# The long sequence's input passes and norm written in front of the last six tiles of the short projection

## The chip, the cores and the metric

The kernel runs on one core of one Trainium2 chip. The metric is the device time of one execution in microseconds, and the number compared is the median of several executions.

## The reference, cut to what matters

Two groups of requests go through the same trunk with shared weights: a long sequence of 1024 positions and a short one of 512, each with 16 meta tokens in front. Only the first part of the layer matters here: the input norm, the combined projection in 18 column tiles of 128, and the attention that reads it.

```
def rms_norm(x, g):
    x32 = x.astype(jnp.float32)
    y = x32 * lax.rsqrt(jnp.mean(x32 * x32, axis=-1, keepdims=True) + NORM_EPS)
    return (y * g.astype(jnp.float32)).astype(x.dtype)

def mixer_sublayer(x, ang_a, ang_b, layer, g_mix, w_in, ...):
    n = rms_norm(x, g_mix)
    proj = n @ w_in                       # 1024 -> 2304 columns
    qa, ka, va, qb, kb, vb = jnp.split(proj, cuts, axis=-1)
    qa = rope_rotate(rms_norm(qa, g_qnorm_a), ang_a)
    ka = rope_rotate(rms_norm(ka, g_knorm_a), ang_a)
    ...                                   # grouped-query attention: 8 heads on 2 K/V heads
    qb = rope_rotate(qb, ang_b)
    kb = rope_rotate(kb, ang_b)
    ...                                   # differential attention: two softmax maps per head
    mix = jnp.concatenate([oa, ob], axis=-1)
    return x + mix @ w_out
...                                       # ConvGLU sublayer, final norm
```

## The kernel before, in words

Activations lie with the feature dimension on the 128 partitions and the positions along the free dimension. The code calls the long sequence s=0 (1040 positions with the meta tokens) and the short one s=1 (528 positions). Every large product runs in three matmul passes on values split in a high and a low part (`mm3`, lines L121, L122, L123: high weight by high x, high weight by low x, low weight by high x), over eight blocks of the contraction, so one product is 24 matmuls. A scheduler decides the order of the instructions on each engine from the order in which the program writes them, taking what is written first when several are ready; each engine then runs its own list strictly in order.

`projection` is a generator that is written once and run for each sequence. It has three parts. First come the input passes, for each of eight feature blocks: a load of x, `xhi` (L234, ScalarE), `xlo` (L235, VectorE), a square (L238, ScalarE) and, for the long sequence, a running sum of the squares in `acc` (L245, GpSimd). Then comes the norm: the first product (`first_ps`, tile KA, first chunk of positions) is written ahead of it, and for each chunk a matmul with `ones_d` sums `acc` over the partitions (L255), ScalarE and VectorE turn it into a reciprocal root (`rsqrt_newton`, L103 to L107) and one VectorE instruction scales all of `rstd` (L257). Only then can the first product leave PSUM, since its eviction `t = ps * rstd` (L312) reads the scaled `rstd`. The long sequence has three chunks, of 384, 384 and 272 positions, the short one two, of 256 and 272. Third come the 18 column tiles, in the order KA, VA, QA, VB, QA+1, ... VB+3, then KB, QB, KB+1, QB+1, ... KB+3, QB+3, with a `yield` after each chunk. The q and k tiles of group A have a norm of their own (L318, L103 to L107, L321) and a rotation, and their results go to memory; those of KB and QB only a rotation.

The program writes the whole projection of the short sequence, then merges two generators: the short sequence's attention and the long sequence's projection, which is to fill TensorE while the softmax of the attention runs. PSUM has two buffers `ps_mm` (long projection: its products, its norm sums, the sums of the head norms, the transposed values), three `ps_s` (products of the short projection, scores of the attention), two `ps_t` and one `ps_o`. The scores are moved out of `ps_s` by VectorE (L433); probabilities are normalised by VectorE (L508), transposed by TensorE (L456) and split again (L114 on ScalarE, L115 on VectorE) before they meet V (L470, L471).

Two orders are forced by hand: the long sequence's input passes stand behind the short sequence's norm (`g.norm_of_short`), and the long sequence's first product stands behind product number 13 of the short projection (`g.short_products`).

Of the kernel before, what the change touches and what calls it, by code (L numbers as in the profile page):

```python
# [74 lines left out]
def behind(g, *ins):  # L75

    es = ExitStack()
    for i in ins:
        es.enter_context(g.tc.issue_after(i))
    return es  # L80
# [13 lines left out]
def pool(ctx, g, name, bufs, side):  # L94
    return ctx.enter_context(g.tc.tile_pool(name=name, bufs=bufs, side=side, reuse_waits="tile"))


def rsqrt_newton(g, tp, out, src, w, eps=None):

    nc = g.nc  # L100
    eps = g.eps if eps is None else eps
    y = tp.tile([P, w], F32, name="rs_y", tag="rs_y", bufs=1)
    nc.scalar.activation(y, src, AF.Ln, bias=eps)  # L103
    nc.scalar.activation(y, y, AF.Exp, scale=-0.5)
    last = nc.scalar.activation(out, y, AF.Square).ins
    nc.vector.scalar_tensor_tensor(out=out, in0=src, scalar=eps, in1=out, op0=ALU.add, op1=ALU.mult)
    nc.vector.scalar_tensor_tensor(out=out, in0=out, scalar=-3.0, in1=y, op0=ALU.add, op1=ALU.mult)  # L107
    return last
# [17 lines left out]
def dense(g, ps, w, xhi, xlo, c0, cw, order=range(KT)):  # L126

    for i, k in enumerate(order):
        last = mm3(g, ps, *block(w, k), xhi[k][:, c0:c0 + cw], xlo[k][:, c0:c0 + cw], i == 0, i == KT - 1)
    return last  # L130
# [66 lines left out]
def projection(ctx, g, s, side, tag, tag2):  # L197
# [9 lines left out]
    xlo = [xp.tile([P, n], F32R, name=f"xlo{k}") for k in range(KT)]  # L207
    rstd = xp.tile([P, n], F32, name="rstd")
    products = []

    def load_tables(which):
        out = []
        for i in range(2):
            tb = xp.tile([P, n], F32, name="rope", tag="rope", bufs=2 if s == 0 else 4)
            nc.sync.dma_start(out=tb, in_=g.rope_in[2 * which + i][:, :n])
            out.append(tb)
        return out
# [3 lines left out]
    with tc.tile_pool(name=f"ps{s}", bufs=2, side=side, reuse_waits="tile") as sp:  # L221
        if s == 1:
            ms = [g.psum.tile(P, cw, tag2) for _, cw in chunks]
        else:
            acc = sp.tile([P, n], F32, name="acc", bufs=1)
        for k in range(KT):
            x = sp.tile([P, n], F32, name="x", tag="x", bufs=2 if s == 0 else 8)
            nc.sync.dma_start(out=x, in_=g.xT[s][k * P:(k + 1) * P, :])
            gk = g.vec[:, V_GMIX + k:V_GMIX + k + 1]
            with ExitStack() as order:  # L230

                for ins in g.norm_of_short:
                    order.enter_context(tc.issue_after(ins))
                nc.scalar.activation(xhi[k], x, AF.Copy, scale=gk)  # L234
                nc.vector.scalar_tensor_tensor(out=xlo[k], in0=x, scalar=gk,  # L235
                                               in1=xhi[k].bitcast(F32), op0=ALU.mult, op1=ALU.subtract)
                sq = acc if k == 0 and s == 0 else x
                nc.scalar.activation(sq, x, AF.Square)  # L238
            if s == 1:
                for ps, (c0, cw) in zip(ms, chunks):  # L240
                    nc.tensor.matmul(ps, lhsT=g.ones_d, rhs=x[:, c0:c0 + cw], start=k == 0, stop=k == KT - 1)
            elif k:
                for c0, cw in chunks:
                    a = acc[:, c0:c0 + cw]
                    nc.gpsimd.tensor_tensor(out=a, in0=a, in1=x[:, c0:c0 + cw], op=ALU.add)  # L245
        c0, cw = chunks[0]
        first_ps = g.psum.tile(P, cw, tag)
        with behind(g, *g.short_products):
            products.append(dense(g, first_ps, first, xhi, xlo, c0, cw))
        for i, (c0, cw) in enumerate(chunks):  # L250
            if s == 1:
                ps = ms[i]
            else:
                ps = g.psum.tile(P, cw, tag2)
                nc.tensor.matmul(ps, lhsT=g.ones_d, rhs=acc[:, c0:c0 + cw], start=True, stop=True)  # L255
            last = rsqrt_newton(g, sp, rstd[:, c0:c0 + cw], ps, cw)
        scaled = nc.vector.tensor_scalar(out=rstd, in0=rstd, scalar1=-0.5, scalar2=None, op0=ALU.mult)  # L257
        g.norm_of_short = [last, scaled.ins]
    es = ExitStack()
    bp = pool(ctx, g, f"pb{s}", 2, side)  # L260
    tp = pool(es, g, f"pt{s}", 2, side)
# [106 lines left out]
    for i in range(4):  # L368
        for j in (KB + i, QB + i):
            w = load_weight(g, wp, g.w_in[j], ahead=1 + s, lo_engine=nc.gpsimd if s == 0 else None)  # L370
            for c0, cw in chunks:
# [3 lines left out]
                    follow()  # L375
                rotary(j, c0, cw, ps, *tab)
                yield 24 * cw
    if s == 1:

        g.short_products = products[13:14]  # L380


def attention(ctx, g, s, side):
# [191 lines left out]
def add_square(g, tp, acc, h, j, c0, cw, eng, bufs=2):  # L575

    nc = g.nc
    hs = h[:, j, c0:c0 + cw]
    if j == 0:
        nc.scalar.activation(acc, hs, AF.Square)  # L580
    else:
        sq = tp.tile([P, cw], F32, name="sq", tag="sq", bufs=bufs)
        nc.scalar.activation(sq, hs, AF.Square)
        eng.tensor_tensor(out=acc, in0=acc, in1=sq, op=ALU.add)
# [163 lines left out]
def conv_glu(ctx, g, s, st, side, wp, wb, gb):  # L748
# [20 lines left out]
    for f0 in range(0, NFF, G):  # L769
# [59 lines left out]
        def finish(c0, acc, sums):  # L829
            rs = rstd[:, 1 + c0:1 + c0 + cw]  # L830
            if sums:
                rsqrt_newton(g, op, rs, acc, cw)
            else:
                mean_rsqrt(g, op, rs, acc, cw)
            for k in range(KT):
                y = op.tile([P, ob, cw], F32, name="y", tag="y", bufs=YB if s == 1 else 4) if k % ob == 0 else y
                hs, gk = h[:, k, 1 + c0:1 + c0 + cw], g.gain[:, V_GFIN + k:V_GFIN + k + 1]
                if k % 4 == 3:
                    nc.scalar.activation(y[:, k % ob], hs, AF.Copy, scale=gk)
                    nc.gpsimd.tensor_tensor(out=y[:, k % ob], in0=y[:, k % ob], in1=rs, op=ALU.mult)  # L840
                else:
                    nc.vector.scalar_tensor_tensor(out=y[:, k % ob], in0=hs, scalar=gk, in1=rs,
                                                   op0=ALU.mult, op1=ALU.mult)
                if (k + 1) % ob == 0:
                    (nc.gpsimd if s == 1 else nc.sync).dma_start(out=yv[:, k + 1 - ob:k + 1, c0:c0 + cw], in_=y)

        waiting = None
        for c0 in range(0, N, cw):
# [3 lines left out]
            for j in range(KT):  # L852
# [5 lines left out]
                else:  # L858
                    add_square(g, op, acc, h, j, 1 + c0, cw, nc.gpsimd if j < PADD else nc.vector, ob)
                if j == LAG and waiting:  # L860
                    finish(*waiting)
# [372 lines left out]
def merge(a, wa, b, wb, ahead=0.0):  # L1234

    done = [float(ahead), 0.0]
    while True:
        i = 0 if b is None or done[0] / wa <= done[1] / wb else 1
        try:
            done[i] += next((a, b)[i])  # L1240
        except StopIteration:
            if i == 0:
                break
            b = None


def drain(gen):
    for _ in gen:
        pass


LAG = 5
NPRE = 4
FPRE = 12
# [16 lines left out]
def trunk_kernel(ctx, tc, g):  # L1271
# [67 lines left out]
    g.norm_of_short, g.short_products = [], []  # L1339

    g.splits = []
    with ExitStack() as es:
        drain(projection(es, g, 1, "right", "s", "t"))
    g.splits = None
    with ExitStack() as es0:
        p0 = projection(es0, g, 0, "left", "mm", "mm")
        with ExitStack() as es1:
            merge(attention(es1, g, 1, "right"), R1[0], p0, R1[1])
        drain(p0)
# [92 lines left out]
```

## Time and profile before

| | before |
|---|---|
| device time, median of 3 executions | 2129.21 us (2128.84, 2129.21, 2135.24) |
| the profiled execution: its own time | 2138.1 us |
| the profiled execution: span, first to last instruction | 2136.3 us |
| mean granted TensorE clock | 0.982 of full speed |
| TensorE busy, share of the span | 2051.1 us, 96% |
| VectorE busy | 1724.1 us, 81% |
| ScalarE busy | 1156.8 us, 54% |
| GpSimd busy | 582.7 us, 27% |

The busy shares are means over stages that differ. What is to be read is the stretch from about 117 us, where the last six tiles of the short projection start, to about 200 us, where the merge of the short attention with the long projection is under way. All times in the views are microseconds from the start of the span. In the views PE is TensorE's matmuls, PEld its weight loads, DVE VectorE, ACT ScalarE, POOL GpSimd, and SPq the queue that issues the transfers; PEclk is the granted clock as a share of 2.4 GHz, so 0.50 is 1.2 GHz.

### The profile page before, as it was taken

To read this page: it belongs to the slowest core of one execution; us is meant where nothing else is said; L and a number is where in the kernel's file an instruction comes from. 1 tells how busy PE (TensorE), PEld (TensorE's weight loads), DVE (VectorE), ACT (ScalarE), POOL (GpSimd) and SP (SyncE) were. 2 spreads that over 40 slices of the span, in tenths; PEclk is the share of its full clock that TensorE was granted. 3 is DMA by queue.
4 is the path that set the end of the run, shared out by engine and by line. 5 is a ranking of instruction groups with operands and counts; after the bars stand their busy time and mean duration, and the time that the engine had idled before them with its cause. 6 is when DMAs were issued, how large, how long until landed. Compare 5 with 4: busy or idle time off the path is not lost.

```text
span 2136.3 us, 35264 instructions
## 1 busy us (share of the span) xinstructions
PE 2051.1 (96%) x12302; PEld 1833.1 (86%) x12302; DVE 1724.1 (81%) x3786; ACT 1156.8 (54%) x2253; POOL 582.7 (27%) x534
## 2 busy tenths in 40 slices
PE   6999999999999999999999999979999999999998
PEld 6988888997887999899989999978888777778877
DVE  6878889767879788888988885578878878869886
ACT  6635566544657556666666765345444444435454
POOL 4653233553112000000000000542444444330112
PEclk8999999999999999999999999998999999999999
DMA  7564335456621322223352224986232232247443
GB/s 252 178 198 133 118 110 170 153 182 226 206 84 55 105 75 70 70 85 114 103 188 77 93 88 145 300 256 229 101 109 89 97 115 84 94 166 258 119 126 126
DMA packets 164897, 296.30 MB, mean 139 GB/s; under 512 B 21456, under 2 KB 82672, under 8 KB 164208
## 3 DMA queue, kind: packets, MB, share of 16 engines
q1 hardware_dynamic: 162416, 287.76, 41.6%
q0 software_dynamic: 2304, 6.29, 0.8%
q8 instruction: 97, 1.59, 0.3%
q14 instruction: 80, 0.66, 0.1%
HBM read 211.13 MB, written 82.85 MB: 138 GB/s over the span
## 4 chain that ended last, share of the span: by engine, by line
PE 76%; DVE 12%; DMA 4%; ACT 3%; issue 3%; POOL 1%; SPq 1%; DVEq 0%; ACTq 0%; POOLq 0%
PE ps_mm L121 17%; PE ps_mm L123 17%; PE ps_mm L122 17%; PE ps_t L456 5%; PE ps_s L431 3%; PE ps_s L432 3%; PE ps_s L121 2%; PE ps_s L122 2%; PE ps_s L123 2%; PE ps_o L471 2%; PE ps_o L470 2%; DVE p L433 1%; DVE w_lo L115 1%; DMA m<-oT 1%; DVE acc L979 1%
## 5 line engine op out<-in xcount | busy, mean ns | idle before, releaser
L121 PE MATMUL ps_mm<-xhi,w_hi 128*128 128x258 f32 (+3 forms) x1264 | 383.4, 304 | 12.0 <-ACT xhi L114 3.7
L122 PE MATMUL ps_mm<-xlo,w_hi 128*128 128x258 f32 (+3 forms) x1264 | 379.0, 300 | 0.3 <-POOL xlo L115 0.3
L123 PE MATMUL ps_mm<-xhi,w_lo 128*128 128x258 f32 (+3 forms) x1264 | 377.2, 299 | 0.3 <-DVE w_lo L115 0.3
L433 DVE TENSOR_SCALAR_CACHE_REDUCE p<-ps_s 114x344 f32<-114x344 f32 (+4 forms) x562 | 257.6, 488 | 30.2 <-PE ps_s L432 19.1
L114 ACT CAST pt_hi<-ps_t 128x512 fp32r<-128x512 f32 (+6 forms) x360 | 169.3, 483 | 181.0 <-PE ps_t L456 155.2
L121 PEld LDWEIGHTS ps_mm<-xhi,w_hi 128*128 128x128 f32 x1264 | 240.0, 190 | 17.5 <-ACT xhi L114 5.4
L438 ACT ACTIVATE p<-p,nm 114x1040 f32<-114x1040 f32 (+5 forms) x212 | 214.8, 1013 | 72.8 <-DVE nm L436 71.8
L115 DVE TENSOR_TENSOR w_lo<-w_f,w_hi 128x1024 fp32r<-128x1024 f32 (+1 forms) x182 | 192.8, 1067 | 66.2 <-ACT w_hi L114 65.6
L122 PEld LDWEIGHTS ps_mm<-xlo,w_hi 128*128 128x128 f32 x1264 | 240.3, 190 | 1.9 <-POOL xlo L115 0.7
L123 PEld LDWEIGHTS ps_mm<-xhi,w_lo 128*128 128x128 f32 x1264 | 240.0, 190 | 1.2 <-DVE w_lo L115 0.5
L114 ACT CAST w_hi<-w_f 128x1024 fp32r<-128x1024 f32 (+1 forms) x199 | 167.6, 856 | 84.9 <-PE ps_mm L122 57.5
L115 DVE TENSOR_TENSOR pt_lo<-ps_t,pt_hi 128x512 fp32r<-128x512 f32 (+4 forms) x312 | 171.7, 561 | 43.7 <-ACT pt_hi L114 42.3
L115 POOL TENSOR_TENSOR a_lo<-gate,a_hi 128x256 fp32r<-128x256 f32 x44 | 43.3, 985 | 545.3 <-ACT a_hi L114 525.9
L431 PE MATMUL ps_s<-k,q 128*114 128x348 f32 (+4 forms) x552 | 183.6, 338 | 3.4 <-DVE p L433 3.2
L456 PE MATMUL ps_t<-ident,p 128*128 128x128 f32 (+7 forms) x1188 | 183.0, 270 | 1.0 <-DVE nm L436 0.5
L432 PE MATMUL ps_s<-k,q 128*114 128x348 f32 (+4 forms) x552 | 171.1, 315 | 0.0
L121 PE MATMUL ps_s<-xhi,w_hi 128*128 128x256 f32 (+4 forms) x480 | 148.7, 313 | 20.4 <-ACT xhi L234 8.2
L456 PEld LDWEIGHTS ps_t<-ident,p 128*128 128x128 f32 (+7 forms) x1188 | 140.4, 136 | 29.6 <-issue 6.8
L123 PE MATMUL ps_s<-xhi,w_lo 128*128 128x256 f32 (+4 forms) x480 | 147.4, 307 | 1.4 <-DMA w_lo<-wo 1.4
L122 PE MATMUL ps_s<-xlo,w_hi 128*128 128x256 f32 (+4 forms) x480 | 148.6, 310 | 0.0
L121 PE MATMUL ps_mm<-t_hi,w_hi 128*128 128x512 f32 (+2 forms) x368 | 144.6, 393 | 1.2 <-DVE v L934 1.2
L123 PE MATMUL ps_mm<-t_hi,w_lo 128*128 128x512 f32 (+2 forms) x368 | 144.4, 392 | 0.1
(275 smaller groups left out, 5309.4 us busy)
## 6 DMA issues: line engine op xcount, KB each, us to landing
w_f<-w_gate SPq DMA_DIRECT2D x46, 512.0 KB, 3.5
w_f<-w_up SPq DMA_DIRECT2D x44, 512.0 KB, 3.4
w_f<-w_in SPq DMA_DIRECT2D x36, 512.0 KB, 3.9
a_f<-act SPq DMA_DIRECT2D x62, 256.0 KB, 2.7
w_f<-w_down SPq DMA_DIRECT2D x22, 512.0 KB, 3.3
act<-a_t SPq DMA_DIRECT2D x44, 256.0 KB, 2.1
a<-w_down SPq DMA_DIRECT2D x40, 256.0 KB, 5.4
w_hi<-wo SPq DMA_DIRECT2D x36, 256.0 KB, 5.1
```

The costliest lines, as they stand in the source:

```text
L114: return (nc.scalar.copy(hi, src).ins, (lo_engine or nc.vector).tensor_tensor(out=lo, in0=src, in1=hi.bitcast(F32), op=ALU.subtract).ins)
L115: (lo_engine or nc.vector).tensor_tensor(out=lo, in0=src, in1=hi.bitcast(F32), op=ALU.subtract).ins)
L121: nc.tensor.matmul(ps, lhsT=whi, rhs=xhi, start=start, stop=False)
L122: nc.tensor.matmul(ps, lhsT=whi, rhs=xlo, start=False, stop=False)
L123: return nc.tensor.matmul(ps, lhsT=wlo, rhs=xhi, start=False, stop=stop).ins
L431: nc.tensor.matmul(ps, lhsT=q[0], rhs=k[:, c0:c0 + cw], start=True, stop=False)
L432: nc.tensor.matmul(ps, lhsT=q[1], rhs=k[:, c0:c0 + cw], start=False, stop=True)
L433: nc.vector.tensor_scalar(out=p[:, c0:c0 + cw], in0=ps, scalar1=HD ** -0.5, scalar2=-3.0e38, op0=ALU.mult, op1=ALU.max, accum_out=mx[:, i: ...
L438: g.last_exp = nc.scalar.activation(p, p, AF.Exp, bias=nm, accum_out=l).ins
L456: nc.tensor.transpose(tps[:, c:c + M], p[:, k0:k0 + kw], g.ident[:M, :M])
L470: nc.tensor.matmul(o, lhsT=v[:, i, :], rhs=hi, start=i == 0, stop=False)
L471: nc.tensor.matmul(o, lhsT=v[:, i, :], rhs=lo, start=False, stop=False)
```

## The change

The generator of the short projection is stopped after 24 chunks (12 of 18 tiles, up to QB). The generator of the long projection is then run up to a new `yield 0` behind its norm, and only then are the last 12 chunks of the short projection written (KB+1, QB+1, ... QB+3). The hand-made order behind product 13 is kept, by another route. What is computed, and by which instructions, stays the same.

```
@@ -207,6 +207,8 @@
     products = []
+    if s == 1:
+        g.short_products = products
...
@@ -245,7 +247,8 @@
         first_ps = g.psum.tile(P, cw, tag)
-        with behind(g, *g.short_products):
+        with behind(g, *(g.short_products[13:14] if s == 0 else [])):
             products.append(dense(g, first_ps, first, xhi, xlo, c0, cw))
...
@@ -256,6 +259,8 @@
         g.norm_of_short = [last, scaled.ins]
+    if s == 0:
+        yield 0
     es = ExitStack()
...
@@ -375,9 +380,6 @@
-    if s == 1:
-        g.short_products = products[13:14]
...
+TN = 24
...
@@ -1339,11 +1342,16 @@
-    with ExitStack() as es:
-        drain(projection(es, g, 1, "right", "s", "t"))
-    g.splits = None
     with ExitStack() as es0:
         p0 = projection(es0, g, 0, "left", "mm", "mm")
+        with ExitStack() as es:
+            p1 = projection(es, g, 1, "right", "s", "t")
+            for _ in range(TN):
+                next(p1)
+            next(p0)
+            drain(p1)
+        g.splits = None
         with ExitStack() as es1:
             merge(attention(es1, g, 1, "right"), R1[0], p0, R1[1])
         drain(p0)
```

In the order of the instructions the engines' lists are the same up to the start of tile KB+1, the first of the last six. They differ from there to the end of the merge, and agree again, but for a few places late in the program, behind it. Two places follow. In the changed program line numbers are a few higher: L255 is L258 there, L257 L260, L312 L317, L321 L326, L273 and L274 L278 and L279, L433 L435, L436 L438. Numbers behind a name are those of the buffers.

The first place is TensorE's list at the end of the short projection. Before, the last matmuls of the short projection (`ps_s_1816`), then the second and third sum of the long norm, then the second product of the long projection:

```order
L121 MATMUL ps_s_1816<-xhi7_172,w_hi_1775 128x272
L122 MATMUL ps_s_1816<-xlo7_180,w_hi_1775 128x272
L123 MATMUL ps_s_1816<-xhi7_172,w_lo_1776 128x272
L255 MATMUL ps_mm_2035<-acc_1940,ones_d_117 128x384
L255 MATMUL ps_mm_2043<-acc_1940,ones_d_117 128x272
L121 MATMUL ps_mm_2152<-xhi0_1914,w_hi_1933 128x384
L122 MATMUL ps_mm_2152<-xlo0_1922,w_hi_1933 128x384
L123 MATMUL ps_mm_2152<-xhi0_1914,w_lo_1934 128x384
```

After the change:

```order
L121 MATMUL ps_s_1961<-xhi7_172,w_hi_1920 128x272
L122 MATMUL ps_s_1961<-xlo7_180,w_hi_1920 128x272
L123 MATMUL ps_s_1961<-xhi7_172,w_lo_1921 128x272
L121 MATMUL ps_mm_2152<-xhi0_1385,w_hi_1404 128x384
L122 MATMUL ps_mm_2152<-xlo0_1393,w_hi_1404 128x384
L123 MATMUL ps_mm_2152<-xhi0_1385,w_lo_1405 128x384
```

The two norm sums have left this place; one now stands right in front of tile KB+1 and the other near the end of its second chunk. The long projection's second product follows the short projection's last at once.

The second place is VectorE's list there. Before, behind the rotation of the last short chunk (`w_1842`), the rest of the long norm, the first product's eviction, then the first evictions of the scores (`p_1891` to `p_2067`) and the second product's eviction:

```order
L274 TENSOR_TENSOR w_1842<-ps_s_1816,rope_300 64x272
L106 SCALAR_TENSOR_TENSOR rstd_1930<-ps_mm_2035,eps_133,rstd_1930 128x384
L107 SCALAR_TENSOR_TENSOR rstd_1930<-rstd_1930,rs_y_2037 128x384
L106 SCALAR_TENSOR_TENSOR rstd_1930<-ps_mm_2043,eps_133,rstd_1930 128x272
L107 SCALAR_TENSOR_TENSOR rstd_1930<-rstd_1930,rs_y_2045 128x272
L257 TENSOR_SCALAR rstd_1930<-rstd_1930 128x1040
L312 TENSOR_TENSOR t_2063<-ps_mm_2002,rstd_1930 128x384
L433 TENSOR_SCALAR p_1891,mx_1892<-ps_s_1893 128x264
L433 TENSOR_SCALAR p_1891,mx_1892<-ps_s_1897 128x264
L433 TENSOR_SCALAR p_2067,mx_2068<-ps_s_2069 128x264
L436 TENSOR_REDUCE nm_1901<-mx_1892 128x1
L312 TENSOR_TENSOR t_2177<-ps_mm_2152,rstd_1930 128x384
```

After the change the rest of the norm and the first eviction stand among the rotations of the last six tiles (`u_` and `w_` are a rotation's parts; `w_lo` is the split of a weight):

```order
L107 SCALAR_TENSOR_TENSOR rstd_1401<-rstd_1401,rs_y_1508 128x384
L277 TENSOR_TENSOR u_1591<-ps_s_1566,rope_298 128x272
L278 TENSOR_TENSOR w_1592<-ps_s_1566,rope_300 64x272
L279 TENSOR_TENSOR w_1592<-ps_s_1566,rope_300 64x272
L115 TENSOR_TENSOR w_lo_1685<-w_f_1682,w_hi_1684 128x1024
L106 SCALAR_TENSOR_TENSOR rstd_1401<-ps_mm_1514,eps_133,rstd_1401 128x272
L277 TENSOR_TENSOR u_1633<-ps_s_1608,rope_298 128x256
L278 TENSOR_TENSOR w_1634<-ps_s_1608,rope_300 64x256
L279 TENSOR_TENSOR w_1634<-ps_s_1608,rope_300 64x256
L107 SCALAR_TENSOR_TENSOR rstd_1401<-rstd_1401,rs_y_1516 128x272
L260 TENSOR_SCALAR rstd_1401<-rstd_1401 128x1040
L317 TENSOR_TENSOR t_2063<-ps_mm_1473,rstd_1401 128x384
```

And this now stands behind the rotation of the last short chunk (`w_1987`):

```order
L279 TENSOR_TENSOR w_1987<-ps_s_1961,rope_300 64x272
L317 TENSOR_TENSOR t_2177<-ps_mm_2152,rstd_1401 128x384
L106 SCALAR_TENSOR_TENSOR hn_2181<-ps_mm_2179,eps_133,hn_2181 128x384
L107 SCALAR_TENSOR_TENSOR hn_2181<-hn_2181,rs_y_2182 128x384
L317 TENSOR_TENSOR t_2338<-ps_mm_2313,rstd_1401 128x272
L435 TENSOR_SCALAR p_2036,mx_2037<-ps_s_2038 128x264
L326 SCALAR_TENSOR_TENSOR t_2063<-t_2063,gain_137,hn_2181 128x384
L435 TENSOR_SCALAR p_2036,mx_2037<-ps_s_2042 128x264
L435 TENSOR_SCALAR p_2067,mx_2068<-ps_s_2069 128x264
L278 TENSOR_TENSOR w_2190<-t_2063,rope_2061 64x384
L279 TENSOR_TENSOR w_2190<-t_2063,rope_2061 64x384
L438 TENSOR_REDUCE nm_2046<-mx_2037 128x1
```

The evictions of the second and third product and the norm of the first k chunk (`hn_2181`, `t_2063`) have moved in front of and in between the first evictions of the scores.

## Rows read from the trace of the kernel before

**Rows 1.** The page, part 1: span, busy time and instructions of each engine.

```profile
span 2136.3 us, 35264 instructions
PE 2051.1 (96%) x12302; PEld 1833.1 (86%) x12302; DVE 1724.1 (81%) x3786; ACT 1156.8 (54%) x2253; POOL 582.7 (27%) x534
```

**Rows 2.** The page, part 4: the chain that ended last, by engine.

```profile
PE 76%; DVE 12%; DMA 4%; ACT 3%; issue 3%; POOL 1%; SPq 1%; DVEq 0%; ACTq 0%; POOLq 0%
```

**Rows 3.** Line L234, the long and short xhi passes: durations, first and last start.

```profile
L234 ACT ACTIVATE xhi<-x,vec x16: 718/942/1165, 7.4 to 72.5; 128x528 fp32r<-128x528 f32 x8, 128x1040 fp32r<-128x1040 f32 x8
```

**Rows 4.** Windows: stretch and length, PE, PEld, DVE, ACT, POOL busy, PEclk, DMA.

```profile
117.20:152.20 35.00, 35.00 (x291) 35.00 (x290) 23.61 (x44) 10.12 (x18) 21.71 (x27) 1.00 0.59 189
...
170.00:190.00 20.00, 16.02 (x85) 13.89 (x85) 19.60 (x60) 11.66 (x27) 9.94 (x11) 0.84 0.42 139
178.00:186.00 8.00, 4.08 (x17) 2.61 (x18) 7.92 (x22) 4.41 (x13) 3.63 (x5) 0.86 0.35 112
184.00:190.70 6.70, 5.74 (x21) 5.26 (x22) 6.42 (x23) 3.86 (x9) 2.41 (x5) 0.51 0.58 198
158.46:163.36 4.90, 4.90 (x15) 4.90 (x16) 1.68 (x3) 0.52 (x1) 0.55 (x3) 0.51 0.91 281
200.00:500.00 300.00, 291.73 (x1912) 273.45 (x1913) 234.91 (x701) 166.35 (x404) 120.22 (x102) 1.00 0.46 146
```

**Rows 5.** Timeline of PE where the short projection ends; in brackets idle time and releaser.

```profile
152.06 0.29 PE L123 MATMUL ps_s<-xhi,w_lo 128*128 128x272 f32 x1
152.19 0.81 PE L255 MATMUL ps_mm<-acc,ones_d 128*128 128x384 f32 x2
155.52 0.70 PE L255 MATMUL ps_mm<-acc,ones_d 128*128 128x272 f32 x2 [2.52 <-DVE rstd L106]
158.46 0.69 PE L121 MATMUL ps_mm<-xhi,w_hi 128*128 128x384 f32 x1 [2.24 <-DVE rstd L106]
158.94 0.52 PE L122 MATMUL ps_mm<-xlo,w_hi 128*128 128x384 f32 x1
```

**Rows 6.** Timeline of ACT there: first and last of the norm's six rows.

```profile
153.04 0.58 ACT L103 ACTIVATE rs_y<-ps_mm,eps 128x384 f32<-128x384 f32 x1 [1.06 <-PE ps_mm L255]
...
157.44 0.43 ACT L105 ACTIVATE rstd<-rs_y 128x272 f32<-128x272 f32 x1
```

**Rows 7.** Timeline of DVE, 154 to 180 us.

```profile
154.76 0.62 DVE L106 SCALAR_TENSOR_TENSOR rstd<-ps_mm,eps,rstd 128x384 f32<-128x384 f32 x1 [0.95 <-ACT rstd L105]
...
159.65 0.56 DVE L312 TENSOR_TENSOR t<-ps_mm,rstd 128x384 f32<-128x384 f32 x1
164.75 0.43 DVE L433 TENSOR_SCALAR_CACHE_REDUCE p<-ps_s 128x264 f32<-128x264 f32 x1 [4.54 <-PE ps_s L432]
...
172.50 2.35 DVE L321 SCALAR_TENSOR_TENSOR t<-t,gain,hn 128x384 f32<-128x384 f32 x1
...
179.08 0.60 DVE L321 SCALAR_TENSOR_TENSOR t<-t,gain,hn 128x384 f32<-128x384 f32 x1
```

**Rows 8.** The chain in order of time, 83 to 85 us: start, length, what.

```profile
83.69 0.17 PE ps_mm L122
83.86 0.18 PE ps_mm L123
84.04 0.65 PE ps_mm L255 x2
```

**Rows 9.** Timeline of PE in the second stall.

```profile
181.35 0.55 PE L339 MATMUL ps_mm<-ident,t 128*128 128x128 f32 x3 [2.30 <-DVE t L333]
...
184.96 0.79 PE L471 MATMUL ps_o<-pt_lo,v 128*128 128x512 f32 x1 [1.36 <-DVE pt_lo L115]
```

**Rows 10.** Timeline of POOL, 159 to 175 us.

```profile
159.95 0.18 POOL L504 CAST halo<-q 128x2 fp32r<-128x2 f32 x1 [4.02 <-DMA q<-qk]
160.75 0.18 POOL L504 CAST halo<-q 128x2 fp32r<-128x2 f32 x1 [0.62 <-DMA q<-qk]
...
171.75 2.68 POOL L115 TENSOR_TENSOR w_lo<-w_f,w_hi 128x1024 fp32r<-128x1024 f32 x1 [6.62 <-ACT w_hi L114]
```

**Rows 11.** Timeline of the transfer queue: the first loads of q.

```profile
156.90 4.79 SPq L402 DMA_DIRECT2D q<-qk  x6
```

**Rows 12.** Waits of PE, 150 to 520 us: total, times, longest.

```profile
PE ps_s L431 <- DVE p L433: 2.8, 6, 1.1
```

More of the change, by code (lines that the diff above doesn't have):

```diff
@@ L209, in projection @@
     products = []
+    if s == 1:
+        g.short_products = products
     def load_tables(which):
@@ L247, in projection @@
         first_ps = g.psum.tile(P, cw, tag)
-        with behind(g, *g.short_products):
+        with behind(g, *(g.short_products[13:14] if s == 0 else [])):
             products.append(dense(g, first_ps, first, xhi, xlo, c0, cw))
@@ L258, in projection @@
         g.norm_of_short = [last, scaled.ins]
+    if s == 0:
+        yield 0
     es = ExitStack()
@@ L377, in projection @@
                 yield 24 * cw
-    if s == 1:
-        g.short_products = products[13:14]
 def attention(ctx, g, s, side):
@@ L1249, in drain @@
         pass
+TN = 24
 LAG = 5
@@ L1341, in trunk_kernel @@
     g.splits = []
-    with ExitStack() as es:
-        drain(projection(es, g, 1, "right", "s", "t"))
-    g.splits = None
     with ExitStack() as es0:
         p0 = projection(es0, g, 0, "left", "mm", "mm")
+        with ExitStack() as es:
+            p1 = projection(es, g, 1, "right", "s", "t")
+            for _ in range(TN):
+                next(p1)
+            next(p0)
+            drain(p1)
+        g.splits = None
         with ExitStack() as es1:
```

## The prediction

> **What bounds the kernel now.** I read the page first. TensorE is busy for 96% of the span [rows 1], and the chain that ended last runs over it for 76%, with VectorE second at 12% [rows 2]. So time is won where TensorE stands still or runs slowly, and work of other engines costs something only where TensorE waits for it.
>
> Next I cut the stretch around the change into windows [rows 4]. In the 35 us of the last six short tiles (117.20 to 152.20) TensorE is busy throughout at the full clock, while VectorE has 35.00 - 23.61 = 11.4 us free and ScalarE 24.9. Right behind comes a first stall. The timeline of TensorE [rows 5] shows it: the last short matmul starts at 152.06, a norm sum follows at 152.19, then 2.52 us of idle, the last norm sum, 2.24 us of idle, and only at 158.46 the second product of the long projection. Both gaps end with a VectorE `rstd` row. The reader should see why: two `ps_mm` buffers exist, the first product holds one until `rstd` is scaled, and so each norm sum, and then the second product, has to wait until the sum before it has gone through ScalarE and L106. In the same 4.90 us that follow (158.46 to 163.36) the granted clock is 0.51, the 1.2 GHz level [rows 4].
>
> There is a second stall from 178 to 186: TensorE busy 4.08 of 8 us, VectorE 7.92, and then from 184.00 to 190.70 the clock is again 0.51 [rows 4]. Its gaps wait for VectorE, 2.30 us for the eviction of a v product and 1.36 us for a split of probabilities [rows 9]. VectorE is 98% busy from 170 to 190 [rows 4] yet stood idle for 4.54 us just before 164.75 [rows 7]: it is a backlog, begun late. From 200 to 500 TensorE loses only 300.00 - 291.73 = 8.3 us, at the full clock.
>
> **What moves.** The title promises more than the lists show. The last of the 16 `xhi` passes starts at 72.5 us [rows 3], some 45 us ahead of tile KB+1, and its place doesn't change. What moves is the second and third chunk of the norm, the scaling of `rstd`, and the first product's eviction: two sums on TensorE, six rows on ScalarE, six on VectorE. No instruction is added or removed.
>
> *On ScalarE and VectorE.* The six ScalarE rows from 153.04 to 157.44 add up to 2.97 us [rows 6], the six VectorE rows from 154.76 to 159.65 to 3.75 us [rows 7]. They now lie beside the last six tiles, whose free time is 11.4 us on VectorE. Cost nothing, covered by three `ps_s` buffers. The wait that is queued there: the rotations and the split `w_lo` of the next weight stand behind L106, which waits for ScalarE. If that cover fails, a tile's low-weight matmul comes late by at most the moved 3.75 us in all; I take 0.
>
> *On TensorE.* A sum of 384 columns costs 0.65 us inside a busy stretch [rows 8], one of 272 columns by its width 0.65 x 272/384 = 0.46. The short projection so ends 1.1 us later. In its place the 6.27 us from 152.19 to 158.46 go away [rows 5]. Net -6.27 + 1.11 = **-5.2 us**.
>
> *The clock behind the first stall.* In the 4.90 us at 1.2 GHz 15 matmuls started [rows 4]; at the full clock such a one takes 0.17 to 0.18 us on the chain [rows 8], 15 x 0.175 = 2.6. Without the idle ahead of it I expect the full clock: **-2.3 us**. The bound on the other side is 0, if something else makes TensorE idle there.
>
> *The second stall.* It costs 8.00 - 4.08 = 3.9 us of idle and half of the 5.74 busy microseconds at 1.2 GHz, 2.9: together 6.8 [rows 4]. VectorE now reaches the merge 3.75 us of work lighter, and the second and third product's evictions and the first k norm fill time in which it was idle. But TensorE also arrives earlier and asks earlier. Between 0 and -6.8 I take half, **-3.4 us**.
>
> *New waits.* With the gap gone, what is late next? First the loads of q. They follow the last short rotation's stores on the transfer queue, and the first needed 159.95 - 156.90 = 3.05 us until GpSimd could read it [rows 10, 11]. Shifted by 1.1 us, both halves of q are there at about 161.9. TensorE has two products in hand meanwhile: 24 x 0.175 = 4.2 us, and 24 x 0.175 x 272/384 = 3.0 us, with a head norm's sum of 0.65 between: from 153.3 to 161.2. That leaves a wait of some 0.7 us, the lower bound. Second, VectorE's list now puts the k norm's L326 (L321 before) between the first evictions of the scores. That row took 2.35 us at 172.50 while GpSimd's `w_lo` ran from 171.75 for 2.68 us, and 0.60 us at 179.08 [rows 7, 10]: 1.75 us lost. Before, three scores were already out of PSUM by then; now two of them wait behind it. As an upper bound I take the two gaps of the second stall once more, 2.30 + 1.36 = 3.7 us [rows 9]. The lock is the nearest row: **+1.7 us**.
>
> The Trainium skill, page "SBUF — State Buffer", section "SBUF: two separate sides", gives the reason why such a pair can't run together: VectorE with two inputs in SBUF and GpSimd reading SBUF use one port pair, locked for a whole instruction, and the other blocks. By that rule the lock comes back whenever the long weight's split lands on the k norm, and the sum stands; were it wrong here, the sum would be 1.7 us better. The rows at 171.75 and 172.50 agree with it.
>
> Sum: -5.2 - 2.3 - 3.4 + 1.7 = -9.2, say **-9 us**. The profiled execution took 2138.1 us, 9 more than the median of 2129.2; the difference is carried over to the median as it is: **2120 us**. Behind 520 us the lists agree again but for a few places, so a lead won by then should last to the end.
>
> **Rivals.**
> *The second stall stays.* VectorE is the bound of the merge's start, and TensorE, arriving early, waits for it as long as before. For it: 98% busy from 170 to 190. Against it: those 4.54 us of idle on VectorE, and the 3.75 us taken from it. Then -5.2 - 2.3 + 3.7 = -3.8, 2125 us, within 0.3%. Chance 0.27.
>
> *The gain is hidden or given back.* The lead could be spent where the merge ends, if the short attention's last blocks bound that place rather than TensorE's sum of work. Against it: no more than 8.3 us of idle in 300 from 200 on [rows 4]. Then about 0 to -2, 2128 us. Chance 0.06.
>
> *Slower: scores stuck behind the head norms.* On VectorE evictions, k and q norms and rotations are now mixed from the first block on, and with three `ps_s` buffers TensorE stops at each late eviction. Such a wait was there 6 times from 150 to 520 us, 1.1 us at the longest [rows 12]. The place is 162 to 220 us, some 14 blocks of scores with two evictions each. With the second stall unchanged, 5.2 + 2.3 = 7.5 us are eaten by 7 waits of 1.1 us; from 13 on it is slower by over 0.3%, 14.3 - 7.5 = 6.8, 2136 us. For it: L326 and two rotation rows between three evictions. Against it: TensorE's list has a product to run between the scores. Chance 0.07.
>
> **How the numbers follow.** A difference of 0.3%, 6.4 us, is about the least that a measurement of this kernel can tell from none: the limits are 2122.8 and 2135.6 us. The forecast, second stall shortened, has a chance of 0.60 and its own range from -5.2 - 2.3 - 6.8 + 0.7 = -13.6, 2115.6, to -5.2 - 2.3 + 1.7 = -5.8, 2123.4. The range for 8 in 10 takes in the first two rivals and, for the scatter of executions (6 us between the three), 2 us at either end: 2113 to 2130. Nearly all of the forecast is faster, and a little of the second-stall rival: 0.60. Same: the two rivals of no great effect, 0.32. Slower: 0.08.
>
> **What would show it right or wrong.** In the changed kernel's timeline the long projection's second product should start within 0.2 us of the short projection's last matmul, without a `rstd` row as releaser, and the clock there stay at 1.00. The last six tiles should take 36.1 us instead of 35.0, with TensorE still busy throughout; gaps there that end with `w_lo` would break the cover. The first scores should start near 162 us. Between 165 and 195 TensorE's idle and the time at 0.5 should be half of before, and the evictions L435 the releaser of few waits. The prediction fails if the windows from 160 to 220 show as much idle and slow clock as before, or if the lead at 200 us is gone by 520.

## The result, and the profile after

| | before | changed |
|---|---|---|
| device time, median of 20 executions | 2130.14 us (2124.91 to 2135.41) | 2138.93 us (2132.87 to 2142.98) |
| the profiled execution | 2138.1 us | 2132.87 us |
| ratio of the medians' runs | | 1.0035, 95% interval 1.0027 to 1.0043 |

The changed kernel is slower, by 1.0035, which is 7.5 us; a second measurement beside other runs gave 1.0040 (1.0026 to 1.0053). The prediction said 9 us faster. The sign is wrong.

The two profiled executions say the opposite of the medians, and a reader who only laid the pages side by side would be misled. The page of the changed kernel, part 1:

```profile
span 2131.0 us, 35265 instructions
...
PE 2045.2 (96%) x12302; PEld 1828.9 (86%) x12302; DVE 1735.7 (81%) x3786; ACT 1156.5 (54%) x2253; POOL 583.3 (27%) x534
```

That span is 5.3 us shorter than the one of before [rows 1], because this execution is the fastest of its kernel and the profiled one of before is slower than all 20 timed ones. One row does point the right way: VectorE has the same 3786 instructions and is busy for 11.6 us longer.

What can be compared is stretches. Both kernels issue 12302 matmuls, so the nth matmul marks the same amount of work. Times between such marks, from TensorE's start times; "again" is a second profile of the same program:

```
matmul from-to           659-953  953-1009  1009-1159  1159-3030  3030-3500  3500-7000  7000-end
before                      35.8      16.6       30.0      293.6       85.1      522.7    1026.8
before, again               35.8      16.9       30.1      295.0       82.9      522.7    1024.4
changed                     36.4       8.9       29.8      304.2       85.0      522.7    1020.3
changed, again              36.4       8.9       30.5      305.3       84.9      522.7    1022.2
```

Matmuls are counted from 0. Nearly all of the last six short tiles lies in 659 to 953, their end and the first stall in 953 to 1009, the second stall in 1009 to 1159, and the rest of the merge runs to 3030. The first stall is gone (16.6 to 8.9). The rest of the merge is 10 us longer, where nothing was expected. Behind 7000 the changed kernel is 2 to 7 us shorter in these four profiles, against the medians; over the profiles of all whole kernels below, the same work takes 1020.3 to 1029.3 us there, so nothing is read from that stretch.

The timeline of TensorE in the changed kernel, where [rows 5] showed the first stall:

```profile
151.59 0.29 PE L123 MATMUL ps_s<-xhi,w_lo 128*128 128x272 f32 x1
151.72 0.34 PE L121 MATMUL ps_mm<-xhi,w_hi 128*128 128x384 f32 x1
...
160.42 0.64 PE L433 MATMUL ps_s<-k,q 128*128 128x264 f32 x3 [0.36 <-DMA q<-qk]
```

The long product follows the short one at once, and the scores wait 0.36 us for q. Windows of the changed kernel (columns as in [rows 4]): matmuls 659 to 953, the place of the first stall, the start of the merge, and 200 to 500:

```profile
113.10:149.50 36.40, 36.40 (x296) 36.06 (x295) 28.86 (x51) 13.45 (x26) 21.50 (x26) 1.00 0.57 187
...
152.20:160.00 7.80, 7.79 (x49) 7.01 (x47) 2.74 (x6) 2.50 (x6) 1.98 (x3) 1.00 0.73 224
160.00:180.00 20.00, 15.75 (x77) 14.20 (x77) 18.77 (x53) 9.53 (x21) 12.04 (x17) 0.83 0.67 228
...
200.00:500.00 300.00, 288.40 (x1844) 271.27 (x1843) 240.21 (x693) 163.98 (x399) 117.24 (x100) 0.96 0.43 139
```

Up to 160 us it goes as predicted: six tiles without a gap, full clock. From 200 to 500 TensorE's clock is 0.96 where it was 1.00 [rows 4], it started 1844 matmuls instead of 1912, and VectorE is busy for 240.21 us instead of 234.91 with 8 instructions fewer.

### The profile page after: what moved, and what is told of

It is laid out like the page before. It is cut to its first block, busy times and chain, and to the rows that moved or that the text cites. A ratio compares the mean times of both kernels' runs of the same rounds, so it can differ in the third digit from the quotient of the medians.

```text
span 2131.0 us, 35265 instructions
## 1 busy us (share of the span) xinstructions
PE 2045.2 (96%) x12302; PEld 1828.9 (86%) x12302; DVE 1735.7 (81%) x3786; ACT 1156.5 (54%) x2253; POOL 583.3 (27%) x534
## 4 chain that ended last, share of the span: by engine, by line
PE 60%; DVE 10%; issue 2%; DMA 2%; ACT 2%; SPq 0%; POOL 0%; DVEq 0%; ACTq 0%
PE ps_mm L121 14%; PE ps_mm L123 14%; PE ps_mm L122 14%; PE ps_t L458 4%; PE ps_s L433 2%; PE ps_s L434 2%; DVE w_lo L115 2%; PE ps_o L473 1%; DVE p L435 1%; PE ps_o L472 1%; DVE acc L981 1%; PE ps_s L122 1%; DMA m<-oT 1%; PE ps_s L123 1%; PE ps_s L121 1%
## 5 line engine op out<-in xcount | busy, mean ns | idle before, releaser
L435 DVE TENSOR_SCALAR_CACHE_REDUCE p<-ps_s 114x344 f32<-114x344 f32 (+4 forms) x562 | 258.0, 488 | 27.8 <-PE ps_s L434 14.3
L433 PE MATMUL ps_s<-k,q 128*114 128x348 f32 (+4 forms) x552 | 184.0, 338 | 5.3 <-DVE p L435 4.6
```

Of the source, the lines that this page charges most:

```text
L433: nc.tensor.matmul(ps, lhsT=q[0], rhs=k[:, c0:c0 + cw], start=True, stop=False)
L435: nc.vector.tensor_scalar(out=p[:, c0:c0 + cw], in0=ps, scalar1=HD ** -0.5, scalar2=-3.0e38, op0=ALU.mult, op1=ALU.max, accum_out=mx[:, i: ...
```

## The experiments

The order in which each engine runs its instructions comes out of a scheduler, and the diff changes it far beyond the lines it moves: with the norm's own rows left aside, 2010 of TensorE's matmuls, 688 of VectorE's and 379 of ScalarE's instructions stand at another place, nearly all in the merge. So the first runs separate the move from the order.

### The order, written out

Each kernel below has this at the end of the program, with a literal for the order wanted (every instruction behind the one before it on its engine, which adds no wait):

```
+    pin(g)
+def pin(g):
+    for row in ORDER:                      # one row for each engine
+        for ins, prev in zip(row[1:], row):
+            g.tc.add_manual_dep(ins, prev.name, <issue order only>)
```

The control, the order of before on the kernel before:

> The kernel before, with the order in which each engine runs its instructions written out: the same program as before. It is the control for the two runs beside it. Every theory: the same time as before, within 0.2% (2126 to 2134 us). A difference of more than 0.2% would mean that writing the order out costs something by itself.

Measured: 2129.92 us, ratio 1.000 (0.9988 to 1.0013). Writing an order out costs nothing that this measurement can tell.

The norm early, all else in the order of before:

> The changed kernel's norm (its rows stand in front of the last six tiles of the short projection, as in the changed kernel), but every other instruction of the program in the order of the kernel before. Theory A, the loss comes from the new order of the merge on all engines: the first stall is gone and nothing is given back, so it is faster than before by 3.8 to 9 us (2121 to 2126 us). Theory B, the moved norm itself costs more than the stall it removes (it holds up the last six short tiles or locks the shared port): as slow as the changed kernel, 2136 to 2141 us. Theory C, a lost clock stretch returns wherever the order puts it, and the place of the norm decides nothing: within 3 us of before.

Measured: 2131.26 us, 1.0008 (0.9998 to 1.0017): level with before, so theory C by the number, and neither A nor B as stated. The moved norm costs no 7 us (B falls), but it wins nothing either. The timeline of TensorE says why:

```profile
156.17 0.33 PE L121 MATMUL ps_mm<-xhi,w_hi 128*128 128x384 f32 x1
163.27 1.00 PE L433 MATMUL ps_s<-k,q 128*128 128x264 f32 x3 [6.76 <-DMA q<-qk]
```

The scores stand directly behind the start of the next product in this order, and q does not arrive before 163. The first stall was covered twice, by the wait for `rstd` and by the wait for q. Of the orders run here, only those that put whole products ahead of the scores used the time. The move and the new order belong together.

The norm late, all else in the order of the changed kernel:

> The kernel before's norm (behind the short projection), but every other instruction of the program in the order that the changed kernel has. Theory A: it keeps the first stall and has the loss of the new order too, so it is slower than before by 9 to 16 us (2139 to 2146 us). Theory B: the norm is where it was, so the time is that of before, within 3 us. Theory C: within 3 us of before.

Measured: 2150.25 us, 1.0095 (1.0075 to 1.0114). Slower, as A said, but by more, and for a reason of its own: VectorE stood idle for 8.77 us in front of L106, ahead of rows that the short tiles need, so 659 to 953 took 47.9 us. What counts is 1159 to 3030: 304.6 us, as in the changed kernel, with the norm where before has it. For the run with the norm early in the order of before it is 294.8. The slow merge goes with the order, not with the norm.

The changed kernel again, which gave the second profile above:

> The changed kernel once more, for a second profile of it, since the first was of its fastest execution: 2136 to 2141 us, 1.002 to 1.005 of before by every theory. What is looked at is where its half-clock stretches lie: theory A expects them again between 200 and 400 us at the same matmuls as in the first profile, theory C expects them elsewhere.

Measured: 2137.77 us, 1.0040. TensorE's gaps of over 0.9 us between 200 and 380 stand at the same matmuls as in the first profile (1307, 1631, 1934, 1939, 2223), so theory A holds here and theory C, which expected other places, does not.

### Both orders, one behind the other

> The changed kernel, with the order on every engine written out: what the changed kernel started up to 160 us in its profile (the moved norm, the last six short tiles, the second and most of the third long product) in its order, and everything later in the order of the kernel before. In the changed kernel the stretch of the first stall (matmul 959 to 1009) took 8.2 us where before had 15.9, with the kernel before's order behind the moved norm it took 17.2 (the scores waited 6.8 us for q). Theory A, the new order of the merge behind that place is what costs: the 7.7 us are won and kept, 2121 to 2126 us. Theory C, TensorE is held by the arrival of q and by VectorE's backlog wherever the two products stand: within 3 us of before, 2128 to 2134. Theory B, the moved rows themselves cost: 2134 us or more.

> The same with the place of change at 192 us, behind the second stall: up to there the changed kernel's order, behind it the order of the kernel before. At that place (matmul 1159) the changed kernel was 7 us ahead of before in both of its profiles. Theory A: the lead stays, 2121 to 2126 us. Theory C: the lead is lost in the 200 us behind it by waits and clock stretches that come back in another place, 2128 us or more.

Measured: 2128.78 us, 0.9991 (0.9982 to 1.0001), and 2130.91 us, 0.9995 (0.9985 to 1.0005). In both profiles 1159 to 3030 is back at 294.0 and 297.0 us and 953 to 1009 stays at 8.9. So by the stretches the merge did what theory A says, and yet the whole kernel kept next to nothing, which is theory C's time. The kernels below that end early look for the rest.

### The norm still later

```
-TN = 24
+TN = 34                                    # the other run: 35
```

> The changed kernel with the norm written two products (one weight tile) before the end of the short projection instead of twelve. The order that comes out differs in the merge both from before and from the changed kernel, on TensorE in about 4000 rows. Theory A: the time goes with the order, so it is another time, anywhere from 2118 to 2150 us, with other gaps at other places, and not between the two. Theory B, the place of the norm decides: between before and the changed kernel, 2130 to 2138 us.

> The same with the norm one product before the end of the short projection. Again another order of the merge. Theory A: another time than either kernel and than the run beside it, anywhere from 2118 to 2150 us. Theory B: close to before, 2129 to 2134 us.

Measured: 2133.57 us, 1.0010 (1.0002 to 1.0019), and 2134.06 us, 1.0014 (1.0005 to 1.0023). Inconclusive between the theories, since the times lie in both ranges or at the edge of one. By the programs' lists, and with the norm's sums left aside, the norm written 22, 24, 26, 28, 29, 31 or 33 products in gives TensorE the changed kernel's order of the merge to the last row, 34 and 35 give two other orders, and behind all 36 it is the order of before. One product more or less can turn the whole merge over.

### Cut off at the end of the merge, and of the attention

The same kernels with their order written out, ended early; the cut for the merge:

```
         drain(p0)
-    es1, es_x, es_h, x = ExitStack(), ExitStack(), ExitStack(), {}
-    ...
...
+    pin(g)
```

> The kernel before up to the end of the merge of short attention and long projection, with its order written out; everything behind it (the attention of the long sequence, the output projections, the feed-forward parts) is left out. It is what the three runs beside it are compared with, by the difference of their medians. In the full profiles the merge's last product stands near 500 us, so some 505 to 525 us.

> The changed kernel with the same part left out. Full kernels: 7 us slower than before. Theory A, the merge's own order costs what the full kernel lost: 5 to 8 us longer than the cut kernel before. Theory D, the merge costs only what single profiles show (from matmul 200 to 3030 442.0 and 444.5 us against 438.7 and 440.8) and the rest is lost behind it: 1 to 5 us longer.

> The moved norm with everything else in the order of the kernel before, with the same part left out. Theory A and theory D: within 2 us of the cut kernel before (the full kernels were 1.3 us apart, and the profiles show 441.7 us from matmul 200 to 3030).

> The changed kernel's order to 192 us and the kernel before's behind it, with the same part left out. Its full profile was 434.4 us from matmul 200 to 3030 where before had 438.7 and 440.8, but its median in full was that of before. Theory D, the lead is real at the merge's end and lost behind it, by half-clock stretches that come at other places: 4 to 7 us shorter than the cut kernel before. Theory C, the single profile was a lucky one and the lead is not there: within 2 us.

> The kernel before up to the end of the long sequence's attention, with its order written out; what is left out: the rest of the short sequence's feed-forward part, and the long sequence's output projection and feed-forward part. It is what the three beside it are compared with, by medians. In the full profiles the attention ends near 1100 us, so 1100 to 1130 us.

> The changed kernel with the same part left out. At the merge's end it was 4.1 us behind, in full it is 7.5 us behind. Theory D1, the rest is lost where the merge hands over to the long attention (matmul 3030 to 3500): 6.5 to 9 us behind. Theory D2, it is lost behind the attention: 3 to 5 us behind.

> The moved norm with everything else in the order of the kernel before, the same part left out. At the merge's end 2.1 us behind, in full 0.4 to 1.3 us behind. Both theories: 0 to 3 us behind.

> The changed kernel's order to 192 us, the kernel before's behind it, the same part left out. At the merge's end 4.4 us ahead, in full level with before. Theory D1: the lead is gone at the attention's end, within 2 us of the cut kernel before. Theory D2: it is still there, 3 to 6 us ahead.

Medians, and the difference to before:

```
                              end of the merge   end of the attention   whole kernel
before                           514.24             1174.66               2130.14
changed                          518.36  +4.1       1181.81  +7.2          +7.5
norm early, order of before      516.31  +2.1       1178.46  +3.8          +1.7
changed to 192, then before      509.86  -4.4       1172.63  -2.0          -1.1
```

(The last column is the ratio times 2130.) For the changed kernel 4.1 us are lost by the merge's end, inside theory D's range and short of theory A's, and the rest by the attention's end: D1. Part of it is the handover, 3030 to 3500: 84.9 to 87.1 us in its three profiles of that stretch, 82.8 to 85.1 in three of before: by their means about 2 us, with ranges that touch. For the mixed order the 4.4 us are real at the merge's end and are lost about half before and half behind the attention's end, which fits neither theory alone. The norm early in the order of before is 3.8 us behind at the attention's end, outside the 0 to 3 us that both theories gave it. The executions of one kernel scatter by 2 to 4 us, so these last steps are not resolved.

### The split in four

What makes the new order slow? In the changed kernel's longest wait between 200 and 300 us TensorE stands still from 211.74 to 213.89. VectorE, GpSimd and TensorE there:

```profile
210.15 0.55 DVE L278 TENSOR_TENSOR w<-t,rope 64x384 f32<-64x384 f32 x1
210.71 2.65 DVE L279 TENSOR_TENSOR w<-t,rope 64x384 f32<-64x384 f32 x1
213.40 0.44 DVE L317 TENSOR_TENSOR t<-ps_mm,rstd 128x272 f32<-128x272 f32 x1
...
210.59 2.37 POOL L115 TENSOR_TENSOR w_lo<-w_f,w_hi 128x1024 fp32r<-128x1024 f32 x1 [0.44 <-ACT w_hi L114]
...
213.89 0.45 PE L121 MATMUL ps_mm<-xhi,w_hi 128*128 128x384 f32 x1 [2.15 <-DVE t L317]
```

L278 and L279 are twins; one takes 0.55 us, the other 2.65, because GpSimd began the split of the next long weight 0.12 us ahead of it. The eviction L317 stands behind it, and the next product waits for its buffer. TensorE's clock from 1.3 us behind that wait on (a window of the changed kernel):

```profile
215.20:218.70 3.50, 3.50 (x14) 3.50 (x13) 3.50 (x14) 2.35 (x7) 1.25 (x3) 0.52 0.73 281
```

Here such a row costs a wait and then half the clock for some 3.4 us. Rows of VectorE over 1.8 us that overlap a split, from 953 to 3030: 2 in both profiles of before; 8 and 9 in those of the changed kernel; 2 in the mixed orders. The splits are as many and about as long in both, 16 of some 2.4 us. The test is to make the split shorter and leave the order alone:

```
-    passes = split(g, hi, lo, w, lo_engine)
...
+        nc.scalar.copy(hi, w)
...
+        for c in range(0, D, D // 4):
+            cc = slice(c, c + D // 4)
+            passes.append(lo_engine.tensor_tensor(out=lo[:, cc], in0=w[:, cc], in1=hi[:, cc].bitcast(F32),
+                                                  op=ALU.subtract).ins)
```

> The kernel before, its order written out, with each GpSimd split of a long weight done in four instructions of a quarter of the columns, one behind the other in the same place. Theory L, such a split holds up a VectorE row for its whole length and that is what the new order multiplies: only two rows of the merge are held up in before (2.35 us at 171.91, 2.31 at 205.03), so it gains little, 0 to 4 us, 2126 to 2130. Theory M, the order itself makes TensorE wait, whatever the split does: 2128 to 2132.

> The changed kernel with the same four short splits. Theory L: the rows of 1.9 to 2.9 us on VectorE are gone from the merge, the waits of TensorE behind them too (2.15 us at 213.89), and it comes to within 3 us of the run beside it, 2128 to 2133. Theory M: still 6 to 9 us slower than the run beside it, 2135 to 2140.

Measured: 2131.20 us, 0.9998 (0.9984 to 1.0013), and 2133.33 us, 1.0005 (0.9995 to 1.0015). The difference of the two orders falls from 7.5 to about 2 us, as theory L said and M denied for the changed kernel. In the kernel before the 0 to 4 us of gain that L allowed did not show. The same place, in the changed kernel with the split in four (the lines have moved by 9):

```profile
210.55 0.55 DVE L287 TENSOR_TENSOR w<-t,rope 64x384 f32<-64x384 f32 x1
211.12 1.03 DVE L288 TENSOR_TENSOR w<-t,rope 64x384 f32<-64x384 f32 x1
212.18 0.44 DVE L326 TENSOR_TENSOR t<-ps_mm,rstd 128x272 f32<-128x272 f32 x1
...
210.99 3.14 POOL L185 TENSOR_TENSOR w_lo<-w_f,w_hi 128x256 fp32r<-128x256 f32 x4 [0.45 <-ACT w_hi L181]
...
212.67 0.45 PE L121 MATMUL ps_mm<-xhi,w_hi 128*128 128x384 f32 x1 [0.53 <-DVE t L326]
```

The row takes 1.03 us instead of 2.65 and TensorE's wait 0.53 instead of 2.15. No row over 1.8 us overlaps a split any more; 1159 to 3030 falls from 304.2 and 305.3 us to 298.2, with 10.2 us at half the clock instead of 23.9. VectorE's busy time from 1159 to 3030 falls from 247.3 and 249.1 to 238.3 us (before: 233.8 and 234.4). It doesn't win the whole way back: before has 293.6 and 295.0 there. No wait of TensorE from 953 to 3030 ends with `w_lo` in the changed kernel, so it is not that `w_lo` is ready sooner.

How the rows that are held up turn into time is less plain than one of them suggests. From 1159 to 3030, from the profiles:

```
                               rows held up   TensorE idle   at 1.2 GHz   stretch
before / again                     1 / 1        8.3 / 7.9     0 / 6.8    293.6 / 295.0
changed / again                    7 / 8       10.5 / 11.8  23.9 / 23.9  304.2 / 305.3
norm late, order of changed          7            13.9         13.7          304.6
norm 34 products in                  7            12.3          3.4          297.6
norm 35 products in                  7            10.4         10.2          300.0
before, split in four                0             7.5         10.2          295.7
changed, split in four               0             9.9         10.2          298.2
```

With the split in four TensorE's idle time hardly falls, and two of the changed kernel's five longer gaps stay as they were (at matmul 1939 1.38 and 1.37 us, at 2223 1.14 us in both); what falls is the time at 1.2 GHz. And with the norm 34 products in there are as many held-up rows as in the changed kernel, the same row among them, for 2.65 us, with the same wait behind it, but the clock stays full:

```profile
211.99 2.65 DVE L279 TENSOR_TENSOR w<-t,rope 64x384 f32<-64x384 f32 x1
...
215.17 0.44 PE L121 MATMUL ps_mm<-xhi,w_hi 128*128 128x384 f32 x1 [2.16 <-DVE t L317]
...
216.50:220.00 3.50, 3.50 (x20) 3.01 (x20) 3.50 (x14) 2.60 (x8) 1.28 (x3) 1.00 0.72 269
```

So the number of held-up rows sets no price by itself. Why the same wait is followed by half the clock in one order and not in the other was not tested. Over all timed executions the mean granted clock was 0.982 and 0.983 in the changed kernel's two measurements, and 0.985 in before and, to within 0.0005, in both kernels with the split in four.

## Why the prediction was wrong

| term of the sum | predicted | measured |
|---|---|---|
| first stall, the sums ahead of it, the clock behind it (659 to 1009) | -7.5 | -7.3: 45.3 and 45.3 against 52.4 and 52.7 |
| second stall and the new waits (1009 to 1159) | -1.7 | +0.1: 29.8 and 30.5 against 30.0 and 30.1 |
| the rest of the merge (1159 to 3030) | 0 | +10.5: mean 304.75 against 294.3 |
| the handover (3030 to 3500) | 0 | about +2 |
| the long attention (3500 to 7000) | 0 | 0.0: 522.7 in all four |

*The first stall* was right to a few tenths: net -5.2 and the clock's -2.3, the second product 0.13 us behind the last short matmul, the clock at 1.00, the scores at 160.4 and 162.2 us for 162. The prediction had also priced the arrival of q behind the two products, 0.7 us; it was 0.36 and 1.43. What it had not seen is that q covers the whole gap a second time where those products do not stand there: that only the new order made the term possible was shown by the run in the order of before.

*The moved rows* cost nothing under the six tiles beyond the two sums: TensorE was busy for 36.40 of 36.40 us.

*The second stall* was to be halved, against 1.7 us of new waits. It was replaced instead: a wait of 1.28 us for `p` at 169.74 and one of 2.17 us for `p` at 172.67 stand where the 2.30 and 1.36 us of [rows 9] were. That is the first rival's "stays".

*The step that failed* is the rest of the merge, put at 0 by the sentence that "a lead won by then should last to the end"; it measured +10.5 us. That sentence rested on the 8.3 us that TensorE loses from 200 to 500 [rows 4], which is a property of the order of before. The lists had shown that all engines' order differs there, and no term was given to that. Behind it stands the lock between VectorE and GpSimd. The prediction saw it ([rows 7, 10], L321 at 172.50 beside `w_lo` at 171.75), priced it once, at 1.7 us, bounded it by 3.7, and counted it only at the merge's start. Sixteen splits run in the merge, and how many of them hold up a VectorE row differs by the order: 2 in before, 8 or 9 in the changed kernel. The split in four, with the order left alone, takes the ratio from 1.0035 (1.0027 to 1.0043) to 1.0005 (0.9995 to 1.0015), some 6 of the 7.5 us, so most of the loss needs the long splits. The step from a held-up row to lost time is shown only in part: of the 10.5 us TensorE's idle time makes some 3 (means 11.2 against 8.1), the rest is longer busy time with 23.9 us at 1.2 GHz against 0 and 6.8; and with 7 held-up rows in this stretch the norm 34 products in is at 1.0010. What remains of the slower merge, 298.2 against 293.6 and 295.0, was not separated further: TensorE is idle there for 9.9 us against 8.3 and 7.9, and 10.2 us at 1.2 GHz against 0 and 6.8.

The rule that the prediction cited, of the Trainium skill's page "SBUF — State Buffer", section "SBUF: two separate sides", that whichever of the two starts first holds the shared ports for a whole instruction, is borne out by the four pieces: the row that took 2.65 us beside a pass of 2.37 us takes 1.03 us behind the first piece, of 0.74 us. The section also names VectorE's instructions in a two-port mode. The rows fit that: `p<-p,r` (L508), with one tensor in SBUF, was among the held-up ones in before, 2.18 us at 205.53 beside a split that began at 205.02, against 0.49 us at 204.00; in which mode it ran, no row shows.

The rival for "slower" had the sign but not the mechanism: it expected the loss from 162 to 220 us, by scores stuck at some 13 evictions. Most of it lies behind that, and TensorE's waits are few, 1 to 2 us each, with the clock behind them.

*Left open:* the terms of the table add up to 5.3 us, some 2 short of the 7.5; the handover's 2 us, which stay with the split in four (86.8 us against 84.1); why the clock falls behind some waits and not behind others; and where the mixed orders lose a lead of 4.4 us that is there at the merge's end. No version was found that beats before beyond the measurement; the nearest, changed to 160 us and before's order behind, is at 0.9991 (0.9982 to 1.0001).

## What to carry to other kernels

Where a scheduler sets the order, a diff of a few lines can be a change of the whole stage: compare the lists first, and if a stage's order differs, price the stage anew instead of carrying its old idle time over. To tell the move from the order, write the order out and cross the two. A wait that two things cover is won only when both go; ask what would have released the engine next. And a collision seen once in a trace is to be counted over every pair that can meet, here 16 splits, before it is priced; the count alone is no price, since the same held-up row and the same wait cost half the clock in one order and nothing of it in another.

## What the runs showed of the hardware that was not expected

Beside a GpSimd pass of 2.37 us over 128x1024 a VectorE row of 0.55 us took 2.65 us; with the pass in four pieces GpSimd takes 3.14 us there but the same row only 1.03. TensorE's longer gaps from 1159 to 3030 in the changed kernel are 0.9 to 2.2 us, not all of them from such rows, yet it spent 23.9 us of that stretch at the 1.2 GHz level where before spent none and 6.8 us in its two profiles: in both profiles of the changed kernel the clock fell behind nearly every one of these gaps. With the norm 34 products in, gaps of the same length at the matmuls 1307 and 1631 were followed by no fall. One profile each was misleading by some 14 us (5.3 us in favour of the changed kernel where the medians say 8.8 against): the matmul number as a ruler, and a second profile, put that right.
